# Second layer's gate and up weights in 2 MB tiles, and the context's last expert sums moved into the second layer

## The chip, the cores and the metric

The kernel runs on one core of a Trainium2 chip. The metric is the device time of one execution in microseconds (us); lower is better. Before the change the median of three runs is 1419.86 us (1418.0 to 1425.77). Five engines take part: TensorE (PE in the profile, its weight loads PEld), VectorE (DVE), ScalarE (ACT), GpSimd (POOL) and SyncE (SP), which issues most DMAs.

## The reference, cut to what matters

Two layers over 512 latent tokens and 256 context tokens of width 1024. Each layer normalises, projects, runs three kinds of heads, projects back, and then runs 16 experts, each of which picks 64 latent and (in the first layer alone) 32 context tokens. The second layer doesn't update the context: it only reads it, in its input projection.

```python
def ec_ffn(h, router_w, w_gate, w_up, w_down):
    n_tok, d = h.shape[1], h.shape[2]
    cap = EC_CAPACITY_FACTOR * n_tok // N_EXPERTS
    aff = jax.nn.softmax((h @ router_w).astype(jnp.float32), axis=-1)
    top_aff, idx = lax.top_k(jnp.swapaxes(aff, 1, 2), cap)
    xg = jax.vmap(lambda hb, ib: hb[ib])(h, idx)
    hid = jax.nn.silu(jnp.einsum('becd,edf->becf', xg, w_gate)) * jnp.einsum('becd,edf->becf', xg, w_up)
    y = jnp.einsum('becf,efd->becd', hid, w_down) * top_aff[..., None].astype(h.dtype)
    return jax.vmap(lambda yb, ib: jnp.zeros((n_tok, d), yb.dtype).at[ib.reshape(-1)].add(yb.reshape(-1, d)))(y, idx)

def hybrid_layer(xl, xc, ...):
    hl = rmsnorm(xl, norm1_g) * (1 + sc1) + sh1
    hc = rmsnorm(xc, norm1_g) * (1 + csc1) + csh1
    l_cq, l_ckv, ... = split_columns(hl @ w_in)
    c_cq, c_ckv, ... = split_columns(hc @ w_in)
    ...                                             # heads, w_o, gated residual
    xl = xl + g2 * ec_ffn(rmsnorm(xl, norm2_g) * (1 + sc2) + sh2, router_w, w_gate, w_up, w_down)
    if update_ctx:
        xc = xc + cg2 * ec_ffn(rmsnorm(xc, norm2_g) * (1 + csc2) + csh2, ...)
    return xl, xc
```

All is float32. An expert's gate and up weights are 1024 x 512 each (2 MB), its down weights 512 x 1024 (2 MB), so a layer's experts read 96 MB.

## The kernel before

**Stages of a layer.** Norm and transposed columns of the input (`hcols`), 15 input projections of 128 columns (`proj`, weights split into two parts of reduced precision by `win`), attention, output projection with routing (`wo_half`, `route_half`), then a loop over 16 experts. PE's order is the order of the code; the other engines' instructions are placed by a list scheduler.

**Weight tiles.** All weights pass through one cycle of tiles of 1 MB (8 KB a partition), handed out in turn by `slot`: three always (`ringa`), more in stages where memory is free. The second layer's experts have 3 + 9 (`RING_B`, from the end of attention) + 7 (`RING_D`, from the end of the output projection) = 19 of them. A gate or up matrix takes two tiles, a down matrix two, an expert six. A tile is loaded again as soon as its last reader is done; the loads stand in SP's queue in a fixed order, and a load whose tile isn't free holds up those behind it. In the second layer the down weights of expert 1 are issued by POOL.

**The expert loop.** Pass e of the loop runs, on PE: gates and ups of expert e (`gate_up`, 32 matmuls, gate and up of the same 128 rows in turn), the transposes of the hidden values of expert e-1, in even passes the transposes of gathered rows (`columns`), eight `cb` matmuls that add an earlier pair of experts to the latents, and `down` of expert e-1. POOL gathers the rows of two experts at once (`xg<-tabx`, one buffer).

**From the first layer to the second.** Experts 14 and 15 of the first layer are summed from memory on the chip, not with a DMA: eight pieces of the latents (`cb<-yp`) and four of the context (`cb<-yc`). Their context outputs are collected in a tile `y`, which `split` cuts into two parts `yc`. Then the second layer normalises its six blocks of 128 tokens, latents (2 to 5) before context (0 and 1), `L302` to `L309`: ACT squares and sums, DVE scales and adds epsilon (`rs_t`), POOL takes the power -1/2 (`rs_r`), DVE multiplies (`xt`, `xc`). `first_blocks` (`L369`) follows: per step of 128 rows two column groups (a transpose on PE into one of two `tp` buffers, scale and shift on ACT, a split into two parts) and six matmuls of the first two projections. The sixteen column groups are eight of the latents and eight of the context.

Of the kernel before, what the change touches and what calls it, by code (L numbers as in the profile page):

```python
# [9 lines left out]
F32 = mybir.dt.float32  # L10
# [9 lines left out]
D = 1024  # L20
# [16 lines left out]
RING_B = (3, 9)  # L37
RING_D = (8, 7)
# [6 lines left out]
def hybrid_kernel(ctx: ExitStack, tc: tile.TileContext, a, out):  # L45
# [36 lines left out]
    def more_slots(es, name, n, before, **kw):  # L82

        p = pool(es, name, n, **kw)
        at = len(cycle) - before
        cycle[at:at] = [p] * n
        return p

    def fewer_slots(p):
        cycle[:] = [c for c in cycle if c is not p]  # L90
# [144 lines left out]
    def layer(li, ada):  # L235
# [40 lines left out]
        with ExitStack() as es2:  # L276
# [25 lines left out]
            for tb in order:  # L302
                src = xt[tb]
                if not upd:
                    src = X["xc"][tb] if tb < CB else X["xl"][tb - CB]
                sq = small.tile([128, 1], F32, name="ssq")
                S.activation(hT[1][:, 0:2, 0:512], src.rearrange("p (a b) -> p a b", a=2), AF.Square, accum_out=sq)
                r = rstd_of(sq, 1, 1.0 / D)
                V.tensor_scalar(xt[tb], src, r[:, 0:1], None, op0=OP.mult)  # L309
            outs = pool(es_o, f"outs{li}", side="right")  # L310
# [57 lines left out]

            def first_blocks():  # L369
# [18 lines left out]
            first_blocks()  # L388
# [351 lines left out]
        if upd:  # L740
            xp = pool(xres, "xl", side="right")
            X["xl"] = [xp.tile([128, D], F32, name=f"xl{i}") for i in range(4)]
            X["xces"] = ExitStack()
            xp = pool(X["xces"], "xc", side="right")
            X["xc"] = [xp.tile([128, D], F32, name=f"xc{i}") for i in range(2)]
            for n, src in (("xl", "x"), ("xc", "ctx")):
                for i, t in enumerate(X[n]):
                    Q.dma_start(t, a[src][i * 128:(i + 1) * 128, :])
        es_b = ExitStack()
        ringb = more_slots(es_b, f"ringb{li}", RING_B[li], 3, side="right")  # L750
# [4 lines left out]
        def load_gu(e, q=Q):  # L755
            wgu = wgus[e] = []
            for w in ("exp_w_gate", "exp_w_up"):
                ws = []
                for k in range(0, KD, 4):
                    t = slot([128, 4, FF])  # L760
                    q.dma_start(t, a[w][li, e, k // 4])
                    ws += [t[:, i] for i in range(4)]
                wgu.append(ws)
# [198 lines left out]
        ringd = more_slots(es_d, f"ringd{li}", RING_D[li], len(cycle))  # L962
# [94 lines left out]
        def down(e, r):  # L1057
# [34 lines left out]
            if e == in_dram:  # L1092
                Y[r] = ex.tile([128, D], F32, name=f"y{r}", bufs=1)
            for q in range(np_):
                V.scalar_tensor_tensor(Y[r][i * rows:(i + 1) * rows, q * n:(q + 1) * n], ps[rows * q:rows * (q + 1), :n],
# [3 lines left out]
        def places(r, g):  # L1099

            nt = NL if r == 0 else NCX
            pl = ex.tile([128, nt], F32R, name=f"pl{r}", bufs=2 - r)
# [3 lines left out]
        def split(g):  # L1106

            o = [ex.tile([128, D], F32R, name=f"yc{i}", bufs=1)[64:128] for i in range(2)]
            parts(Y[1][64:128], o, S.copy)
            pl = places(1, g)[64:128]  # L1110
            return [(pl, [y[:, hf * 512:(hf + 1) * 512] for hf in range(2)]) for y in o]

        def combine(r, terms):

            def piece(tb, hf):
# [3 lines left out]
                x = X["xl" if r == 0 else "xc"][tb][:, hf * 512:(hf + 1) * 512]  # L1119
                V.tensor_tensor(x, x, ps, op=OP.add)  # L1120

            for tb in range(len(streams[r])):
# [8 lines left out]
        def finish(e, r):  # L1131
# [77 lines left out]
        fewer_slots(ringb)  # L1209
        fewer_slots(ringd)  # L1210
# [21 lines left out]
def arrays_of(inputs):  # L1232
# [77 lines left out]
```

## Time and profile before

| | us |
|---|---|
| median of three runs | 1419.86 |
| the profiled execution | 1423.59 |
| its span, first to last instruction | 1421.8 |
| PE busy | 1278.7 (90% of the span) |
| DVE busy | 704.3 (50%) |
| ACT busy | 512.0 (36%) |

Around the span lie 1.8 us. PE is the busiest engine, but a busy PE in this profile is not a PE at its peak, and the two places that the change touches have other limits: one is the passage between the layers (about 820 to 860 us from the span's start), the other the second layer's experts (about 1184 us to the end), where the DMA engines are busy throughout.

### The profile page before, as it was taken

To read this page: it belongs to the slowest core of one execution; us is meant where nothing else is said; L and a number is where in the kernel's file an instruction comes from. 1 tells how busy PE (TensorE), PEld (TensorE's weight loads), DVE (VectorE), ACT (ScalarE), POOL (GpSimd) and SP (SyncE) were. 2 spreads that over 40 slices of the span, in tenths; PEclk is the share of its full clock that TensorE was granted. 3 is DMA by queue.
4 is the path that set the end of the run, shared out by engine and by line. 5 is a ranking of instruction groups with operands and counts; after the bars stand their busy time and mean duration, and the time that the engine had idled before them with its cause. 6 is when DMAs were issued, how large, how long until landed. Compare 5 with 4: busy or idle time off the path is not lost. (4 is left out here: it accounts for less than half of the span.)

```text
span 1421.8 us, 21561 instructions
## 1 busy us (share of the span) xinstructions
PE 1278.7 (90%) x8582; PEld 809.6 (57%) x8582; DVE 704.3 (50%) x1554; ACT 512.0 (36%) x1089; POOL 216.4 (15%) x252
## 2 busy tenths in 40 slices
PE   3989989989999959999999969989999968999995
PEld 0768866657678833444444348876778754343332
DVE  1545256566753452333333473847776351333345
ACT  2523145454543322222222252436666332232222
POOL 1111000313120230111111121101232011111111
PEclk9989999999999969999999969998999989999998
DMA  9523416435661398999999811110016458999993
GB/s 362 191 89 119 146 55 235 180 137 188 258 242 43 151 315 325 381 373 378 373 375 376 335 58 59 45 63 1 2 37 254 170 198 322 419 420 419 420 421 121
DMA packets 54309, 321.95 MB, mean 226 GB/s; under 512 B 8561, under 2 KB 8689, under 8 KB 20673
## 3 DMA queue, kind: packets, MB, share of 16 engines
q1 hardware_dynamic: 45664, 286.75, 51.6%
q0 software_dynamic: 8544, 33.82, 7.5%
q8 instruction: 68, 1.11, 0.3%
q14 instruction: 33, 0.26, 0.1%
HBM read 304.52 MB, written 16.02 MB: 225 GB/s over the span
## 5 line engine op out<-in xcount | busy, mean ns | idle before, releaser
L59 PE MATMUL mm<-slot,xgT 128*32 128x256 f32 (+1 forms) x2048 | 290.9, 494 | 4.3 <-DMA slot<-in_exp_w_up_dram 3.6
L59 PE MATMUL mm<-hT,w 128*128 128x512 f32 (+1 forms) x1176 | 230.3, 355 | 3.1 <-POOL w L135 2.0
L59 PEld LDWEIGHTS mm<-hT,w 128*128 128x128 f32 x1176 | 192.2, 192 | 37.4 <-POOL w L135 2.4
L59 PEld LDWEIGHTS mm<-slot,xgT 128*32 128x32 f32 (+1 forms) x2048 | 104.4, 125 | 178.2 <-issue 143.9
L59 PE MATMUL mm<-slot,hTe 128*32 128x256 f32 (+1 forms) x1024 | 147.0, 489 | 1.2 <-ACT hTe L1053 1.1
L1044 DVE TENSOR_TENSOR gh<-mm,gh 64x512 f32<-64x512 f32 (+1 forms) x48 | 29.0, 604 | 189.2 <-ACT gh L1043 187.7
L1043 ACT ACTIVATE gh<-mm 64x512 f32<-64x512 f32 (+1 forms) x48 | 24.9, 519 | 243.3 <-PE mm L59 155.9
L1013 ACT ACTIVATE xgT<-tp,modT,a 128x64 f32<-128x64 f32 (+1 forms) x192 | 68.9, 426 | 85.7 <-PE tp L1009 82.6
L59 PE MATMUL mm<-wo,mixb 128*128 128x512 f32 x360 | 97.5, 406 | 2.3 <-DVE mixb L135 1.3
L59 PEld LDWEIGHTS mm<-slot,hTe 128*32 128x32 f32 (+1 forms) x1024 | 50.2, 123 | 80.6 <-issue 65.6
L689 ACT COPY pt<-tp 128x512 f32<-128x512 f32 (+1 forms) x120 | 64.9, 542 | 82.9 <-PE tp L686 81.9
L686 PE MATMUL tp<-ident,p 128*128 128x128 f32 x552 | 87.8, 284 | 5.8 <-ACT pt L689 2.6
L676 POOL TENSOR_SCALAR p<-p,sm 128x768 f32<-128x768 f32 (+1 forms) x30 | 58.5, 1950 | 125.8 <-DVE sm L675 117.5
L686 PEld LDWEIGHTS tp<-ident,p 128*128 128x128 f32 x552 | 61.6, 142 | 27.4 <-issue 18.3
L59 PE MATMUL ada<-slot,sT 128*32 128x512 f32 x384 | 53.5, 676 | 23.0 <-DMA slot<-in_ada_w_dram 23.0
L59 PEld LDWEIGHTS mm<-wo,mixb 128*128 128x128 f32 x360 | 64.2, 189 | 16.5 <-DVE mixb L135 2.2
L59 PE MATMUL sc<-kt,qh 96*128 96x512 f32 (+1 forms) x324 | 69.7, 348 | 0.0
L59 PE MATMUL sc<-kst,qst 128*128 128x256 f32 (+1 forms) x288 | 49.4, 304 | 20.4 <-DVE mx L673 12.8
L1120 DVE TENSOR_TENSOR xl<-xl,cb 128x512 f32<-128x512 f32 x72 | 45.8, 683 | 44.4 <-PE cb L59 43.4
L134 ACT CAST w<-slot 128x1024 fp32r<-128x1024 f32 x30 | 31.4, 1047 | 100.1 <-PE mm L59 73.8
L665 DVE TENSOR_REDUCE mx<-sc 128x1 f32<-128x768 f32 (+1 forms) x60 | 51.1, 851 | 26.9 <-PE sc L59 25.9
L996 POOL DMA_INDIRECT xg<-tabx,gidx x24 | 23.2, 968 | 254.9 <-PE tp L1051 150.6
(246 smaller groups left out, 1788.0 us busy)
## 6 DMA issues: line engine op xcount, KB each, us to landing
slot<-in_exp_w_gate_dram SPq DMA_DIRECT2D x62, 1024.0 KB, 18.4
slot<-in_exp_w_up_dram SPq DMA_DIRECT2D x62, 1024.0 KB, 17.6
slot<-in_exp_w_down_dram SPq DMA_DIRECT2D x62, 1024.0 KB, 19.8
slot<-in_ada_w_dram SPq DMA_DIRECT2D x48, 1024.0 KB, 6.7
slot<-in_win_dram SPq DMA_DIRECT2D x14, 1024.0 KB, 7.4
slot<-in_wo_dram SPq DMA_DIRECT2D x8, 1024.0 KB, 4.8
tabx<-xn POOLq DMA_DIRECT2D x10, 512.0 KB, 3.0
xt<-in_x_dram SPq DMA_DIRECT2D x4, 512.0 KB, 4.4
```

The lines of the kernel that those rows point to most:

```text
L59: PE.matmul(o, l, r, start=start, stop=stop, skip_group_check=True)
L134: (hi or V.tensor_copy)(out[0], x)
L665: V.tensor_reduce(mx, sc[:, :n], axis=AX.X, op=OP.max, negate=True)
L676: (G if s and self.kind == "mla" else V).tensor_scalar(p[:, :n], p[:, :n], sm, None, op0=OP.mult)
L686: PE.transpose(ps[:, b * 128:(b + 1) * 128], p[:, (b0 + b) * 128:(b0 + b + 1) * 128], ident)
L689: S.copy(o, ps[:, :n * 128])
L996: G.indirect_dma_start(out=xg, out_offset=None, in_=tabx[li], in_offset=bass.IndirectOffsetOnAxis(ap=gidx[:ng, c:c + 1], axis=0))
L1013: S.activation(xgT[:, k0 + k, :n], ps[:, k * ng:k * ng + n], AF.Identity, bias=b[:, 0:1], scale=s[:, 0:1])
L1043: S.activation(gh[64:128, :n], ps[0:64, :n], AF.Silu)
L1044: V.tensor_tensor(gh[0:64, :n], ps[64:128, :n], gh[64:128, :n], op=OP.mult)
L1120: V.tensor_tensor(x, x, ps, op=OP.add)
```

## The change

Two things change. In the second layer a gate or up matrix is one DMA of 2 MB into a tile of 16 KB a partition, out of a copy of the weights in that layout; these tiles come from a cycle of their own (`wide_slot`), four from the end of attention and two more from the end of the output projection. Down weights and all others stay in 1 MB tiles, of which the second layer's experts now have 3 + 1 + 3. Memory for weights is the same: 19 x 8 KB before, 7 x 8 KB + 6 x 16 KB after. The first layer's experts are left as they were.

The four context pieces of experts 14 and 15 leave the end of the first layer. They run between the steps of the second layer's first two latent projections (`first_latents`), followed by the context's norms; the eight context column groups come after these projections instead of between their steps. The second part of these two projections' weights is formed by DVE and no longer by POOL.

```diff
-RING_B = (3, 9)
-RING_D = (8, 7)
+RING_B = ((3, 0), (1, 4))
+RING_D = ((8, 0), (3, 2))
...
+    def wide_slot(shape):
+        wide.append(wide.pop(0))
+        return wide[-1].tile(shape, F32, name="wslot", tag="wslot")
...
-            for tb in order:
+            def norm(tb, junk):
                 src = xt[tb]
                 if not upd:
                     src = X["xc"][tb] if tb < CB else X["xl"][tb - CB]
                 sq = small.tile([128, 1], F32, name="ssq")
-                S.activation(hT[1][:, 0:2, 0:512], src.rearrange("p (a b) -> p a b", a=2), AF.Square, accum_out=sq)
+                S.activation(junk, src.rearrange("p (a b) -> p a b", a=2), AF.Square, accum_out=sq)
                 r = rstd_of(sq, 1, 1.0 / D)
                 V.tensor_scalar(xt[tb], src, r[:, 0:1], None, op0=OP.mult)
+            for tb in order if upd else order[:4]:
+                norm(tb, hT[1][:, 0:2, 0:512])
...
+            def ctx_sums():
+                def start():
+                    S.copy(X["yc"][0][64:128], X["y"][64:128])
+                    V.tensor_tensor(X["yc"][1][64:128], X["y"][64:128], X["yc"][0][64:128].bitcast(F32), op=OP.subtract)
+                def piece(tb, hf):
+                    ps, cs = psn("ada"), slice(hf * 512, hf * 512 + 512)
+                    for i, y in enumerate(X["yc"]):
+                        mm(ps, X["pl"][64:128, tb * 128:(tb + 1) * 128], y[64:128, cs], i == 0, i == 1)
+                    x = X["xc"][tb][:, cs]
+                    V.tensor_tensor(x, x, ps, op=OP.add)
+                def end():
+                    for tb in range(CB):
+                        norm(tb, tmp(D, "junk").rearrange("p (a b) -> p a b", a=2))
+                return [start] + [lambda tb=tb, hf=hf: piece(tb, hf) for tb in range(CB) for hf in range(2)] + [end]
+            def first_latents():
+                hcols(0, NCX, NT, 0)
+                hcols(0, NCX, NT, 1)
+                ws = [win(i) for i in range(2)]
+                pl = [ps_mm() for _ in ws]
+                sums = ctx_sums()
+                for k in range(KD):
+                    if k + 2 < KD:
+                        hcols(0, NCX, NT, k + 2)
+                    for w, ps in zip(ws, pl):
+                        proj_k(ps, w, k, NCX, NT)
+                    for f in sums[k - 1:k] if k else ():
+                        f()
+                for k in range(KD):
+                    hcols(1, 0, NCX, k)
+                first.update({i: [pl[i], None] for i in range(2)})
...
-            first_blocks()
+            (first_blocks if upd else first_latents)()
...
+            X["y"] = xp.tile([128, D], F32, name="y1")
+            X["yc"] = [xp.tile([128, D], F32R, name=f"yc{i}") for i in range(2)]
+            X["pl"] = xp.tile([128, NCX], F32R, name="pl1")
...
+                if not upd:
+                    t = wide_slot([128, KD, FF])
+                    q.dma_start(t, a[w + "1"][e])
+                    wgu.append([t[:, i] for i in range(KD)])
+                    continue
...
-        def split(g):
-            o = [ex.tile([128, D], F32R, name=f"yc{i}", bufs=1)[64:128] for i in range(2)]
-            parts(Y[1][64:128], o, S.copy)
-            pl = places(1, g)[64:128]
-            return [(pl, [y[:, hf * 512:(hf + 1) * 512] for hf in range(2)]) for y in o]
...
-                    todo.extend(combine(0, pair[-2:]))
-            elif e % 4 == 3:
-                todo.extend(combine(1, split(e // 4)))
+                    todo.extend(combine(pair[-2:]))
+            elif e == NE - 1:
+                places(1, e // 4)
...
+    for n in ("exp_w_gate", "exp_w_up"):
+        a[n + "1"] = i[n][1].reshape(NE, KD, 128, FF).transpose(0, 2, 1, 3)
+        a[n] = a[n][:1]
```

The schedule shows what this moves. First DVE, at the passage between the layers, before and after (`xl` and `xt` are latents, `xc` context, `yc` the parts of the context's sums, `w` projection weights). Before:

```order
L135 TENSOR_TENSOR yc_7059<-y_7014,yc_7058 64x1024
L1120 TENSOR_TENSOR xc_3845<-xc_3845,cb 128x512 x2
L1120 TENSOR_TENSOR xc_3846<-xc_3846,cb 128x512 x2
L141 TENSOR_SCALAR rs_t<-ssq 128x1
L309 TENSOR_SCALAR xt_7139<-xl_3838,rs_r 128x1024
L141 TENSOR_SCALAR rs_t<-ssq 128x1
L309 TENSOR_SCALAR xt_7140<-xl_3839,rs_r 128x1024
```

And after, from the same point, which is the latents' last sum:

```order
L152 TENSOR_SCALAR rs_t<-ssq 128x1
L387 TENSOR_TENSOR yc_3849<-y_3847,yc_3848 64x1024
L320 TENSOR_SCALAR xt_7121<-xl_3838,rs_r 128x1024
L152 TENSOR_SCALAR rs_t<-ssq 128x1
L146 TENSOR_TENSOR w_7192<-slot,w_7191 128x1024
L320 TENSOR_SCALAR xt_7122<-xl_3839,rs_r 128x1024
L146 TENSOR_TENSOR w_7196<-slot,w_7195 128x1024
L152 TENSOR_SCALAR rs_t<-ssq 128x1 x2
L320 TENSOR_SCALAR xt_7123<-xl_3840,rs_r 128x1024
L320 TENSOR_SCALAR xt_7124<-xl_3841,rs_r 128x1024
```

The four context sums no longer stand ahead of the latents' norms; the split of `y` and the two weight splits stand among them.

Next ACT, after the column groups of the latents (`ht<-tp` with 512 columns). `ht<-tp` with 256 columns is a column group of the context, `hT<-ht` its first part, `sqq<-mm` reads a finished projection. Before:

```order
L330 ACTIVATE ht<-tp,modT_1508,a_1_2560 128x256 x2
L134 CAST hT_7135<-ht 128x256 x2
L330 ACTIVATE ht<-tp,modT_1508,a_1_2560 128x256 x2
L134 CAST hT_7135<-ht 128x256 x2
L134 CAST w_7400<-slot 128x1024
L393 ACTIVATE sqq_7391<-mm 128x512
```

And after:

```order
L318 ACTIVATE junk,ssq<-xc_3846 128x1024
L444 ACTIVATE sqq_7393<-mm 128x512
L145 CAST w_7402<-slot 128x1024
L344 ACTIVATE ht<-tp,modT_1508,a_1_2560 128x256 x2
L444 ACTIVATE sqq_7394<-mm 128x512
L145 CAST hT_7117<-ht 128x256 x2
L145 CAST w_7461<-slot 128x1024
L344 ACTIVATE ht<-tp,modT_1508,a_1_2560 128x256 x2
L145 CAST hT_7117<-ht 128x256 x2
L344 ACTIVATE ht<-tp,modT_1508,a_1_2560 128x256 x2
```

All eight context groups now stand behind the finished first projection (`sqq`), with the casts of the next two projections' weights between them; before, they were done when it finished.

Last SP, the loads of the second layer's experts from expert 1's on (`slot` is a 1 MB tile, `wslot` a 2 MB tile, `g2l` the gates of the residual). Before:

```order
L761 DMA slot<-in_exp_w_gate_dram 128x2048
L761 DMA slot<-in_exp_w_up_dram 128x2048
L761 DMA slot<-in_exp_w_gate_dram 128x2048 x2
L761 DMA slot<-in_exp_w_up_dram 128x2048 x2
L761 DMA slot<-in_exp_w_gate_dram 128x2048
L984 DMA g2l<-modrow_87 64x512 x2
L761 DMA slot<-in_exp_w_up_dram 128x2048
L769 DMA slot<-in_exp_w_down_dram 128x2048 x3
```

And after:

```order
L830 DMA slot<-in_exp_w_down_dram 128x2048 x2
L817 DMA wslot<-in_exp_w_up_dram 128x4096
L830 DMA slot<-in_exp_w_down_dram 128x2048 x2
L817 DMA wslot<-in_exp_w_gate_dram 128x4096
L817 DMA wslot<-in_exp_w_up_dram 128x4096
L830 DMA slot<-in_exp_w_down_dram 128x2048
L1046 DMA g2l<-modrow_87 64x512 x2
L817 DMA wslot<-in_exp_w_gate_dram 128x4096
L817 DMA wslot<-in_exp_w_up_dram 128x4096
L830 DMA slot<-in_exp_w_down_dram 128x2048
```

Before, four gates' and ups' tiles of experts 2 and 3 could follow one another as tiles came free; now expert 2's down weights stand ahead of its gates, and one down tile of expert 3 stands on either side of that expert's gates and ups.

## Rows read from the trace of the kernel before

**Rows 1.** Windows; stretch, length, engines' busy us, PE clock, DMA share, GB/s.

```profile
600.00:800.00 200.00, 195.74 (x1760) 83.83 (x1758) 75.25 (x182) 46.62 (x132) 25.10 (x21) 1.00 1.02 377
842.00:844.00 2.00, 2.00 (x9) 1.70 (x8) 1.59 (x3) 0.07 (x2) 0.00 (x0) 0.50 0.00 0
1200.00:1350.00 150.00, 145.86 (x688) 57.76 (x683) 53.21 (x80) 40.69 (x91) 18.00 (x14) 0.99 1.01 420
```

**Rows 2.** PE in order of time, between the layers: start, us, work, idle before.

```profile
839.60 3.44 PE L59 MATMUL mm<-hT,w 128*128 128x512 f32 x6
...
846.80 1.62 PE L59 MATMUL mm<-hT,w 128*128 128x512 f32 x6
...
858.80 16.50 PE L59 MATMUL mm<-hT,w 128*128 128x512 f32 x94 [0.53 <-DVE w L135]
```

**Rows 3.** DVE in order of time, between the layers.

```profile
820.85 0.69 DVE L1120 TENSOR_TENSOR xl<-xl,cb 128x512 f32<-128x512 f32 x1 [0.17 <-PE cb L59]
821.57 1.22 DVE L135 TENSOR_TENSOR yc<-y,yc 64x1024 fp32r<-64x1024 f32 x1
823.38 2.63 DVE L1120 TENSOR_TENSOR xc<-xc,cb 128x512 f32<-128x512 f32 x4 [0.59 <-PE cb L59]
...
826.76 2.84 DVE L309 TENSOR_SCALAR xt<-xl,rs_r 128x1024 f32<-128x1024 f32 x1 [0.69 <-POOL rs_r L142]
...
833.89 0.75 DVE L309 TENSOR_SCALAR xt<-xl,rs_r 128x1024 f32<-128x1024 f32 x1 [0.67 <-POOL rs_r L142]
```

**Rows 4.** POOL in order of time, between the layers.

```profile
826.72 2.33 POOL L135 TENSOR_TENSOR w<-slot,w 128x1024 fp32r<-128x1024 f32 x1
```

**Rows 5.** ACT in order of time, between the layers.

```profile
854.65 1.02 ACT L330 ACTIVATE ht<-tp,modT,a 128x256 f32<-128x256 f32 x2 [0.25 <-DVE hT L135]
855.57 0.71 ACT L134 CAST hT<-ht 128x256 fp32r<-128x256 f32 x2
...
858.36 1.05 ACT L134 CAST w<-slot 128x1024 fp32r<-128x1024 f32 x1
```

**Rows 6.** PE's waits in the second layer's experts: us in total, times, longest.

```profile
PE mm L59 <- DMA slot<-in_exp_w_up_dram: 3.6, 2, 3.0
```

**Rows 7.** PE in order of time, second layer's experts.

```profile
1182.77 1.06 PE L1009 MATMUL tp<-ident,xg 128*128 128x128 f32 x8 [1.79 <-DMA xg<-tabx,gidx]
1183.95 13.95 PE L59 MATMUL mm<-slot,xgT 128*64 128x512 f32 x64
...
1199.37 3.65 PE L59 MATMUL mm<-slot,hTe 128*64 128x512 f32 x16
...
1340.24 8.45 PE L59 MATMUL mm<-slot,xgT 128*64 128x512 f32 x30 [3.00 <-DMA slot<-in_exp_w_up_dram]
...
1370.11 7.08 PE L59 MATMUL mm<-slot,xgT 128*64 128x512 f32 x30 [0.58 <-DMA slot<-in_exp_w_up_dram]
...
1383.17 7.04 PE L59 MATMUL mm<-slot,xgT 128*64 128x512 f32 x32
```

**Rows 8.** DMA queues from 1200 to 1350: packets, MB, share of 16 engines.

```profile
q1 hardware_dynamic: 8203, 59.72, 95.8%
q0 software_dynamic: 864, 3.15, 5.2%
```

**Rows 9.** Windows: four stretches of 4 us at the experts' start.

```profile
1186.00:1190.00 4.00, 4.00 (x20) 1.29 (x18) 0.00 (x0) 1.62 (x2) 0.00 (x0) 1.00 0.65 226
1190.00:1194.00 4.00, 4.00 (x22) 1.42 (x20) 0.69 (x1) 0.59 (x1) 0.00 (x0) 1.00 1.00 412
1194.00:1198.00 4.00, 4.00 (x22) 1.19 (x19) 0.00 (x0) 0.00 (x0) 0.00 (x0) 1.00 0.98 332
1198.00:1202.00 4.00, 3.95 (x25) 1.93 (x26) 0.69 (x1) 3.65 (x10) 0.96 (x1) 1.00 0.93 381
```

**Rows 10.** SP in order of time: the first load after a tile came free.

```profile
1187.63 0.34 SPq L761 DMA_DIRECT2D slot<-in_exp_w_up_dram  x1
```

**Rows 11.** The gathers of the second layer, from issue to landing.

```profile
DMA to landing us min/median/max: 4.3/8.6/8.9
```

More of the change, by code (lines that the diff above doesn't have):

```diff
@@ L80, in slot, with more_slots @@
         return cycle[-1].tile(shape, F32, name="slot", tag="slot")
-    def more_slots(es, name, n, before, **kw):
+    wide = []
+    def wide_slot(shape):
+        wide.append(wide.pop(0))
+        return wide[-1].tile(shape, F32, name="wslot", tag="wslot")
+    def more_slots(es, name, n, before, cyc=cycle, **kw):
+        if not n:
+            return None
         p = pool(es, name, n, **kw)
-        at = len(cycle) - before
-        cycle[at:at] = [p] * n
+        at = len(cyc) - before
+        cyc[at:at] = [p] * n
         return p
     def fewer_slots(p):
-        cycle[:] = [c for c in cycle if c is not p]
+        for cyc in cycle, wide:
+            cyc[:] = [c for c in cyc if c is not p]
     def psn(tag):
@@ L749, in layer @@
         es_b = ExitStack()
-        ringb = more_slots(es_b, f"ringb{li}", RING_B[li], 3, side="right")
+        rings = [more_slots(es_b, f"ringb{li}", RING_B[li][0], 3, side="right"),
+                 more_slots(es_b, f"wideb{li}", RING_B[li][1], 0, wide, side="right")]
         load_wo(1, 1)
@@ L961, in layer @@
         es_d = ExitStack()
-        ringd = more_slots(es_d, f"ringd{li}", RING_D[li], len(cycle))
+        rings += [more_slots(es_d, f"ringd{li}", RING_D[li][0], len(cycle)),
+                  more_slots(es_d, f"wided{li}", RING_D[li][1], len(wide), wide)]
         steps[0]()
@@ L1091, in down @@
             i = e % np_
-            if e == in_dram:
-                Y[r] = ex.tile([128, D], F32, name=f"y{r}", bufs=1)
             for q in range(np_):
-                V.scalar_tensor_tensor(Y[r][i * rows:(i + 1) * rows, q * n:(q + 1) * n], ps[rows * q:rows * (q + 1), :n],
+                V.scalar_tensor_tensor(X["y"][i * rows:(i + 1) * rows, q * n:(q + 1) * n], ps[rows * q:rows * (q + 1), :n],
                                        gw[r][rows * q:rows * (q + 1), e:e + 1], g2[r][rows * q:rows * (q + 1), :],
@@ L1101, in places, with combine @@
             nt = NL if r == 0 else NCX
-            pl = ex.tile([128, nt], F32R, name=f"pl{r}", bufs=2 - r)
+            pl = X["pl"] if r else ex.tile([128, nt], F32R, name=f"pl{r}", bufs=2)
             G.tensor_scalar(pl, tok[:, :nt], slots[r][:, g:g + 1], None, op0=OP.is_equal)
             return pl
-        def split(g):
-            o = [ex.tile([128, D], F32R, name=f"yc{i}", bufs=1)[64:128] for i in range(2)]
-            parts(Y[1][64:128], o, S.copy)
-            pl = places(1, g)[64:128]
-            return [(pl, [y[:, hf * 512:(hf + 1) * 512] for hf in range(2)]) for y in o]
-        def combine(r, terms):
+        def combine(terms):
             def piece(tb, hf):
@@ L1118, in piece @@
                     mm(ps, pl[:, tb * 128:(tb + 1) * 128], ys[hf], i == 0, i == len(terms) - 1)
-                x = X["xl" if r == 0 else "xc"][tb][:, hf * 512:(hf + 1) * 512]
+                x = X["xl"][tb][:, hf * 512:(hf + 1) * 512]
                 V.tensor_tensor(x, x, ps, op=OP.add)
-            for tb in range(len(streams[r])):
+            for tb in range(len(streams[0])):
                 for hf in range(2):
@@ L1208, in layer @@
         es_d.close()
-        fewer_slots(ringb)
-        fewer_slots(ringd)
+        for p in rings:
+            fewer_slots(p)
     ada = []
```

## The prediction

> **What bounds the kernel now.** I read the windows by stage first. The second layer's experts (about 1184 us to the end) have both PE and the DMA engines busy: 145.86 of 150 us on PE, and the DMA engines without a gap at 420 GB/s [rows 1]. PE's waits tell which of the two sets the end: only 3.6 us of waiting for weights in the whole stage, in two waits [rows 6]. PE in order of time shows them at 1340.24 (3.00 us, the gates and ups of expert 12) and at 1370.11 (0.58 us, expert 14); expert 15 starts at 1383.17 without one [rows 7]. So PE sets the pace first, lives on a stock of loaded tiles, and from expert 12 on has none left: PE and DMA end level. The weights arrive at 2.49 us a MB there: expert 12 and expert 14 lie 12 MB apart, and 1370.11 - 1340.24 = 29.87 us. Anything that makes the weights late by more than a microsecond is paid in full at the end; anything that makes them early is worth no more than the two waits, 3.6 us, plus the 1.8 us by which the 30 matmuls after the longer one ran slow (8.45 us against about 6.6, which is 7.04 for 32 scaled down) [rows 7].
>
> The other place is the passage between the layers. DVE adds the latents' last sum at 820.85, and PE has its first projection at 839.60; between lie context sums and norms, one after the other on DVE [rows 2, 3]. From 858.80 on PE runs 94 matmuls without a gap [rows 2]: this is the point at which a gain or loss of the passage is read.
>
> **The change part by part: the passage.** The latents' last sum ends at 821.5, and the four context adds follow from 823.38 [rows 3]. In place of these DVE does, by the new order, a share of the norms at once: the split of the context's sums and two weight splits of the same size at 1.22 each, four norms at 0.75, and small statistics between them, which I put at 0.15 each: 7.3 us, and some 0.6 us for POOL's power. The norms count 0.75 each, not 2.84: the first two of before ran beside POOL's weight split of 2.33 us, which is gone, and the third, without one, took 0.75 [rows 3, 4]. The last latent norm ends at 829.4. The transposes, ACT's column group and DVE's two parts add 2.4 us: first projection at 831.8, 7.8 us earlier than 839.60.
>
> What follows takes that back. The loop has the same 48 matmuls, 0.27 us each (1.62 for six) [rows 2], 13.0 us; six latent column groups of four transposes at about 0.36, 2.2 us; the eight moved context matmuls at 0.27, 2.2 us; and the start at low clock (0.50, the lower of the two levels, while PE was busy all through 842 to 844 [rows 1]; six matmuls 3.44 us there against 1.62 [rows 2]), some 1.3 us: end at 850.5. Before, the loop ended at about 857.5 with all context columns in it. Now they come behind it, alone, through two PSUM buffers. Before the last two find a buffer, ACT's order holds: two weight casts at 1.0, three pairs of groups at 1.0, two pairs of their casts at 0.7 [rows 5], two squares put at 0.5: 7.4 us. PE's stream of the next projection, queued behind these transposes, starts at about 857.9 instead of 858.4 (858.80 less two matmuls that ran earlier), and after 7 us with little work PE starts it at the lower clock: up to 1.8 us. Less about 1.1 us because the clock rises sooner at the start of the loop, this comes to +0.2, and I take 0. Bounds: -6 (the head start of 7.8 kept, less some 2 for the moved matmuls) and +4 (the low clock lasting as it did from 836 to 844, half of 8 us).
>
> **The change part by part: the second layer's experts.** Work on PE, DVE and ACT is the same; the loads differ.
>
> First gather. Tiles for 19 MB stand ready in both versions before expert 0 is through. Before, 12 MB of loads stand ahead of the tiles that come free with the output projection, and 7 MB behind; by the new order 10 ahead (expert 2's down weights stop the queue) and 9 behind. The 2 MB more, 5.0 us at 2.49, are still moving when POOL gathers the first rows. A gather lands after 4.3 us at least and 8.6 in the median [rows 11]; PE waited for this one at 1182.77 [rows 7]. Cost 0 to 4.3; I take 2.
>
> Restart. After the 19 MB the DMA engines stand idle until a tile comes free. Before, that is when half of expert 0's gates and ups is done: SP issues at 1187.63 [rows 10]. The four stretches up to 1202 moved 226, 412, 332 and 381 GB/s [rows 9], as much as 12.9 us at 420, so it is as if a full stream had begun at 1189.1. Now both 2 MB tiles come free when expert 0 is through: 1183.95 + half of 13.95 = 1190.9 [rows 7], plus the 2 of the gather and 0.5 to start: 1193.4. Its 4 MB last 10 us; the next load, a down tile, waits for the first half of expert 0's down matmuls (1199.37 + 1.8 + 2 = 1203.2 [rows 7]), and what is queued behind it on SP, expert 4's gates and ups, waits with it: the stream just holds.
>
> Whole tiles. Counted from the order, before, the first half of expert 14's ups is MB 87 of the stage; the whole of expert 15's ups, which PE now needs before its first matmul, is MB 94 in the new order. Before, MB 87 less the 19 took 1370.11 - 1189.1 = 181.0 us; seven more at 2.49 are 17.4.
>
> Rate. The two queues give two equations: 8203 packets and 59.72 MB took 95.8% of 16 x 150 us, 864 packets and 3.15 MB 5.2% [rows 8]. Their solution is 37.4 us a MB and 8.2 ns a packet. A 2 MB tile saves 144 packets, 0.074 us of 4.99 over 16 engines, 1.5%; the 24 tiles of experts 4 to 15 save 1.8 us. Bounds: no gain, if the packets keep their size; at most 3.6 us, if all 190 us went at 428 GB/s (16 / 37.4); and a loss, for which the nearest row is the first layer's 377 GB/s [rows 1], a stage with scatters beside the loads: 10% on 190 us would be 19 us. Nothing in the change adds such traffic, so I keep only 4 us of loss. The Trainium skill (HBM Reference, Specifications) puts a core that streams alone at about 425 GB/s. By that ceiling the 190 us could shrink by 1.2%, 2.3 us, not 3.6; this trace's 420 lies just under it.
>
> Sum: 1193.4 + 181.0 + 17.4 - 1.8 = 1390.0, less 1.3 for a gather of 0.5 MB that now falls into the idle time = 1388.7, against 1383.17: +5.5. PE's short waits (about 1 us an expert from the tenth on) cost it clock inside time that it waits anyway. Behind expert 15's start nothing changes; its down weights land 5 us later and are needed 15.7 us later.
>
> The sum goes against the profiled execution: 1423.59 + 0 + 5.5 = 1429.1. That execution lies 3.7 us above the median of 1419.86, so I forecast 1425.
>
> **The rivals.**
> *The head start is kept* (-6 + 5.5): 1419. For it: DVE and PE really are through with the latents 6 to 8 us earlier. Against it: ACT's order above, with all eight context groups behind the first finished projection.
> *The weights are never late.* If packets of twice the size bring enough, both waits go: -5.4, 1414.5; with the head start 1409. For it: only 3.6 us of waiting stand between. Against it: the packet's share of 8.2 ns. The Trainium skill (DMA: Bandwidth & Descriptors, Bandwidth) gives 341 GB/s for a DMA of 1 MB and 425 for 16 MB, by which larger DMAs would gain far more; the 2.49 us a MB shows 420 with 1 MB tiles, so that loss isn't there to win.
> *The DMA engines start late* and the kernel gets slower. The first gather lands under full load (8.6): 2.3 more; PE, without work for over 4 us, then runs expert 0 at the lower clock, 1.8 more, and its tiles come free that much later; with no gain in rate, 1.8. 1425 + 5.9 = 1431. It decides from the point at which expert 0's gates and ups end 3 us later than by the sum, apart from what the passage shifts. For it: the 9 MB behind the output projection; against it: the gather shares the engines only for its last part.
>
> **How the numbers follow.** Forecast 0.52 (own range 1420 to 1429), head start kept 0.18, never late 0.09, late start 0.21. A measurement of this kernel tells about 0.5%, 7.1 us, from no change: faster is below 1412.8, slower above 1427.0. Faster: most of never late with some head start, 0.08. Slower: late start 0.19, and the upper part of the forecast, 0.14: 0.33. The rest, 0.59, is within. For 8 in 10 the range goes from the never-late case to above the late start: 1414 to 1434.
>
> **What would show it.** The first projection starts near 832 and the long stream behind the context's columns still near 858; if it begins near 852, the passage's step fails. The DMA engines idle from the landing of the first 19 MB until expert 0's gates and ups end; windows beyond 1210 at 425 to 427 GB/s; PE's waits for gates and ups add to 6 to 9 us in short pieces from expert 10 or 11 on. Windows still at 420 or below, or waits that begin at expert 8 or earlier, would make the forecast too low; no waits at all, too high.

## The result, and the profile after

The changed kernel takes 1435.45 us (median of 4 runs, 1430.7 to 1439.24), the kernel before beside it 1422.13 (4 runs): a ratio of 1.0092, 95% interval 1.0066 to 1.0119. It is slower, by some 13 us, and the forecast of 1425 and its range, 1414 to 1434, both lie below it. The direction and the DMA rate that were named came; the size did not. The profiled execution took 1430.7 us, the fastest of the four, with a span of 1428.9 us.

Executions of one kernel differ by some us before the changed places are reached. So times of the passage are counted below from the end of the latents' last sum on DVE, and times inside the experts from the choice: the two PE transposes of the lists of chosen rows (`tp<-ident,lt`), at 1176.00 in the profile before and at 1174.72 after. Prices of kernels are ratios, put into us at 1421.5.

The passage, PE in order of time (start, us, work, idle time before and its releaser); it answers to [rows 2]:

```profile
830.43 3.02 PE L60 MATMUL mm<-hT,w 128*128 128x512 f32 x6
...
849.12 0.27 PE L342 MATMUL tp<-ident,xc 128*128 128x128 f32 x1
850.60 0.55 PE L342 MATMUL tp<-ident,xc 128*128 128x128 f32 x3 [1.20 <-DVE xc L320]
851.58 1.15 PE L342 MATMUL tp<-ident,xc 128*128 128x128 f32 x4 [0.44 <-ACT ht L344]
854.53 1.15 PE L342 MATMUL tp<-ident,xc 128*128 128x128 f32 x4 [1.81 <-ACT ht L344]
856.40 1.15 PE L342 MATMUL tp<-ident,xc 128*128 128x128 f32 x4 [0.72 <-ACT ht L344]
857.20 19.22 PE L60 MATMUL mm<-hT,w 128*128 128x512 f32 x96
```

The latents' last sum, the zero of this stage, ends at 815.01 + 4.87 = 819.88 (before, at 821.5):

```profile
815.01 4.87 DVE L1173 TENSOR_TENSOR xl<-xl,cb 128x512 f32<-128x512 f32 x8
```

The head start is there: the first projection comes 10.6 us after that sum, not 18.1. The context's columns take it back, waiting for ACT. A window shows what PE pays for that (columns as in [rows 1]):

```profile
852.00:862.00 10.00, 7.47 (x22) 5.29 (x22) 5.25 (x11) 6.77 (x16) 0.00 (x0) 0.50 0.54 210
```

The granted clock is at its lower level from 852 to 862; 96 matmuls take 19.22 us, where 94 took 16.50 [rows 2].

The experts' start, PE, answering to [rows 7]:

```profile
1174.72 0.39 PE L983 MATMUL tp<-ident,lt 16*128 16x16 f32 x2 [11.70 <-DVE lt L979]
...
1183.28 1.94 PE L1071 MATMUL tp<-ident,xg 128*128 128x128 f32 x8 [2.81 <-DMA xg<-tabx,gidx]
1185.15 14.51 PE L60 MATMUL mm<-wslot,xgT 128*64 128x512 f32 x64
```

From the choice to expert 0's columns it is 8.56 us, not 6.77. POOL in order of time says why. First before, then after (no row of either stands ahead of the prediction):

```profile
1163.00 0.58 POOL L858 DMA_DIRECT2D tabx<-xn  x1 [1.49 <-DMA slot<-in_exp_w_gate_dram]
1163.61 1.08 POOL L769 DMA_DIRECT2D slot<-in_exp_w_down_dram  x2
1177.55 1.06 POOL L996 DMA_INDIRECT xg<-tabx,gidx  x1 [12.27 <-DVE gw L939]
```

```profile
1156.11 0.54 POOL L830 DMA_DIRECT2D slot<-in_exp_w_down_dram  x1 [1.92 <-PE tp L928]
...
1159.38 0.58 POOL L830 DMA_DIRECT2D slot<-in_exp_w_down_dram  x1
1160.89 0.54 POOL L919 DMA_DIRECT2D tabx<-xn  x1 [0.93 <-ACT xn L917]
...
1178.92 1.06 POOL L1058 DMA_INDIRECT xg<-tabx,gidx  x1 [16.91 <-issue]
```

`tabx` is the table in DRAM from which rows are gathered; its last 512 KB are written here. Expert 1's two down loads, which POOL issued behind that write, now stand ahead of it. How long the four writes of the stage took to land, before and after:

```profile
DMA to landing us min/median/max: 2.9/3.0/9.2
```

```profile
DMA to landing us min/median/max: 2.9/3.0/17.2
```

The last write lands at 1160.89 + 17.2 = 1178.1, after the choice, and the gather is issued 4.20 us after the choice instead of 1.55. That the gather waited for this write is read from these times; the profile names no releaser (`issue`), and an experiment below tests it. It then lands in 4.2 us (before, 5.1):

```profile
xg<-tabx,gidx POOLq DMA_INDIRECT x1, 4.2
```

SP's first load of a tile that came free, and the windows (for [rows 9, 10, 1]):

```profile
1192.82 0.34 SPq L817 DMA_DIRECT2D wslot<-in_exp_w_gate_dram  x1
```

```profile
1190.00:1194.00 4.00, 4.00 (x22) 1.35 (x20) 0.51 (x1) 0.59 (x1) 0.00 (x0) 1.00 0.18 33
1194.00:1198.00 4.00, 4.00 (x22) 1.32 (x20) 0.18 (x1) 0.00 (x0) 0.00 (x0) 1.00 0.87 340
1198.00:1202.00 4.00, 3.95 (x24) 1.80 (x22) 0.69 (x1) 1.89 (x5) 0.66 (x1) 1.00 1.01 434
1202.00:1210.00 8.00, 8.00 (x40) 2.73 (x38) 2.12 (x3) 3.10 (x8) 0.30 (x1) 1.00 0.99 383
1210.00:1350.00 140.00, 135.92 (x634) 53.55 (x632) 50.86 (x76) 36.44 (x80) 17.43 (x13) 1.00 1.01 425
```

The DMA engines stand nearly idle until expert 0 is through (33 GB/s) and then run at 425 GB/s, but not at once: 340 from 1194 to 1198 and 383 from 1202 to 1210. The queues [rows 8] and PE's waits [rows 6], and the waits in order of time from the first:

```profile
q1 hardware_dynamic: 5495, 60.12, 95.3%
q0 software_dynamic: 864, 3.15, 5.3%
```

```profile
PE mm L60 <- DMA wslot<-in_exp_w_up_dram: 5.1, 6, 1.5
```

```profile
1299.08 7.08 PE L60 MATMUL mm<-wslot,xgT 128*64 128x512 f32 x30 [0.81 <-DMA wslot<-in_exp_w_up_dram]
...
1388.52 1.02 PE L60 MATMUL mm<-wslot,xgT 128*64 128x512 f32 x2
1390.23 7.08 PE L60 MATMUL mm<-wslot,xgT 128*64 128x512 f32 x30 [0.69 <-DMA wslot<-in_exp_w_up_dram]
```

From expert 9 on every expert except expert 14 waits a little. Expert 15's gates and ups end 222.59 us after the choice (1390.23 + 7.08 - 1174.72); before it was 214.21.

### The profile page after: what moved, and what is told of

It reads as the page before. It is cut to its first block, busy times and chain, and to the rows that moved or that the text cites. A ratio compares the mean times of both kernels' runs of the same rounds, so it can differ in the third digit from the quotient of the medians.

```text
span 1428.9 us, 21486 instructions
## 1 busy us (share of the span) xinstructions
PE 1282.0 (90%) x8582; PEld 808.7 (57%) x8582; DVE 702.8 (49%) x1556; ACT 511.3 (36%) x1089; POOL 213.6 (15%) x250
## 5 line engine op out<-in xcount | busy, mean ns | idle before, releaser
L60 PE MATMUL mm<-slot,xgT 128*32 128x256 f32 (+1 forms) x1536 | 173.0, 452 | 1.3 <-DVE xgT L1077 0.7
L60 PE MATMUL mm<-wslot,xgT 128*64 128x512 f32 x512 | 120.3, 596 | 5.1 <-DMA wslot<-in_exp_w_up_dram 5.1
L60 PEld LDWEIGHTS mm<-slot,xgT 128*32 128x32 f32 (+1 forms) x1536 | 66.4, 119 | 98.3 <-issue 70.5
L60 PE MATMUL mm<-wo,mixb 128*128 128x512 f32 x360 | 101.6, 420 | 1.6 <-ACT mixb L145 0.9
L60 PEld LDWEIGHTS mm<-wslot,xgT 128*64 128x64 f32 x512 | 38.0, 138 | 84.5 <-issue 71.9
L60 PEld LDWEIGHTS mm<-wo,mixb 128*128 128x128 f32 x360 | 67.5, 198 | 16.5 <-ACT mixb L145 1.4
## 6 DMA issues: line engine op xcount, KB each, us to landing
slot<-in_exp_w_up_dram SPq DMA_DIRECT2D x30, 1024.0 KB, 14.2
```

The source lines that it names most:

```text
L60: PE.matmul(o, l, r, start=start, stop=stop, skip_group_check=True)
```

## The experiments

The theory after the first comparison had three parts: the passage, whole 2 MB tiles, and the first gather. Its rival for the gather was the prediction's own argument, the 9 MB of loads. All kernels were timed in five rounds beside the kernel before, on three chips, so they are compared by their ratios. "Restart" is SP's first load of a freed tile, "end" the end of expert 15's gates and ups, both in us from the choice, from each kernel's profile.

| kernel | ratio to before, 95% | us | restart | end |
|---|---|---|---|---|
| before | | | 11.6 | 214.21 |
| changed, again | 1.0084 (1.0061 to 1.0108) | +11.9 | 19.0 | 223.42 |
| passage alone | 1.0016 (1.0001 to 1.0031) | +2.3 | 11.6 | 213.67 |
| whole tiles alone | 1.0052 (1.0033 to 1.0071) | +7.4 | 18.8 | 223.54 |
| half tiles alone | 1.0018 (0.9999 to 1.0036) | +2.6 | 14.9 | 216.91 |
| changed, table write by ACT | 1.0057 (1.0039 to 1.0074) | +8.1 | 14.2 | 218.49 |
| half tiles, table write by ACT | 1.0001 (0.9984 to 1.0019) | +0.1 | 10.9 | 211.23 |
| before, table write by ACT | 1.0002 (0.9984 to 1.0020) | +0.3 | 10.8 | 213.04 |
| changed, half tiles and write by ACT | 1.0011 (0.9993 to 1.0030) | +1.6 | 10.8 | 212.67 |
| half tiles, two loads each | 1.0010 (0.9990 to 1.0030) | +1.4 | 11.2 | 214.17 |

**The changed kernel once more**, with no edit.

> The changed kernel once more, for its time on the same chip as the parts and a second trace. If the parts add up: the sum of the two others within 3 us, about +8 to +13 on before. If its trace is again near 1429 us in span while the timed runs lie near 1435, the difference is between executions and not in the two places; if it is near 1435, the stretch that is longer than in the first trace shows where.

1434.35 us (6 runs). The loss is there again, and so is the held gather: its columns start 9.23 us after the choice.

**The passage alone** (against the changed kernel):

```diff
-RING_B = ((3, 0), (1, 4))
-RING_D = ((8, 0), (3, 2))
+RING_B = ((3, 0), (9, 0))
+RING_D = ((8, 0), (7, 0))
...
-                if not upd:
-                    t = wide_slot([128, KD, FF])
-                    q.dma_start(t, a[w + "1"][e])
-                    wgu.append([t[:, i] for i in range(KD)])
-                    continue
```

> The passage alone: the context's last sums and norms are moved as in the change, all weights stay in 1 MB tiles as before. Theory A (the time is lost in the second layer's experts, by late and whole 2 MB tiles, and the passage costs little: the trace of the changed kernel has it 2.8 us longer from the latents' last sum to the end of the second layer's third projection): +1 to +4 us on before. Rival B (the passage is what costs, by context columns alone on ACT and a PE at the low clock behind them): +8 to +13 us. Rival C (the passage is a gain that the experts hide): -2 us or less.

1423.88 us (12 runs). A small loss, just told from none; the experts run as before. The latents' last sum, the passage's zero, ends here at 817.21 + 1.28 = 818.49:

```profile
817.21 1.28 DVE L1168 TENSOR_TENSOR xl<-xl,cb 128x512 f32<-128x512 f32 x2 [0.17 <-PE cb L60]
```

**Whole tiles alone**, on the passage of before (against the kernel before):

```diff
-RING_B = (3, 9)
-RING_D = (8, 7)
+RING_B = ((3, 0), (1, 4))
+RING_D = ((8, 0), (3, 2))
...
+                if not upd:
+                    t = wide_slot([128, KD, FF])
+                    q.dma_start(t, a[w + "1"][e])
```

> The 2 MB tiles alone: weights of the second layer's gates and ups as in the change, the passage as before. Theory A: +6 to +10 us on before; expert 15 starts some 7 us later, counted from the end of the routing, as in the changed kernel. Rival B: +0 to +4 us. Rival C: +9 us or more, more than the whole change.

1429.91 us (8 runs). Most of the loss is here, and the gather is held here too (columns 9.07 us after the choice), so that the cause lies with the tiles and not with the passage.

**Half tiles alone**: 2 MB tiles again, but each with one half of the rows of both gates and ups (against whole tiles alone):

```diff
-                    q.dma_start(t, a[w + "1"][e])
+                    t = wide_slot([128, 2, 4, FF])
+                    q.dma_start(t, a["exp_w_gu1"][e, h])
```

> 2 MB tiles of 16 KB a partition cut the other way: one tile holds rows 0 to 511 of both gate and up, the next rows 512 to 1023 of both; passage as before. PE can start on the first tile and frees it halfway, as with 1 MB tiles. Theory A (lateness by whole tiles costs, the packets of 16 KB are a small gain): 3 to 6 us less than the 2 MB tiles alone, so +0 to +5 us on before. Rival D (the order and number of loads ahead of the first gather cost, not the whole tiles): the same as the 2 MB tiles alone, within 2 us.

1424.39 us (12 runs): 4.8 us less than whole tiles by the ratios. What is left, 2.6, goes with a gather still held (columns 8.60 us after the choice).

**The table's last write by ACT.** In the changed kernel this edit takes the write out of POOL's queue and leaves the order of the weights' loads as it is:

```diff
-                G.dma_start(tabx[li][row:row + 128, :], xn)
+                (S if not upd and tb == tbs[-1] else G).dma_start(tabx[li][row:row + 128, :], xn)
```

> The changed kernel with one difference: the last write of the second layer's table of rows (512 KB, the table from which the experts' rows are gathered) is issued by ACT, which made the rows, and so no longer stands behind expert 1's two down loads on POOL's queue. Theory A (the order on POOL's queue holds the first gather back: 17.2 us from issue to landing of that write against 9.2 before): the write lands 3 to 9 us after its issue, the first gather is issued about 1.6 us after the transposes of the choice's rows instead of 4.2, expert 0's columns start 6.8 us after them instead of 8.6 to 9.2, expert 2 starts 27 to 28 us after them instead of 29.9 to 30.8, and the kernel ends 2 to 3 us earlier than the changed one: 1431.5 to 1433. Theory B (it is the 9 MB of loads behind the output projection, as the prediction had it): the write or the gather lands as late as now whatever its queue, expert 0 starts no earlier, and the time stays within 1 us of the changed kernel's 1434.4.

1429.09 us (11 runs): 3.8 to 5.0 less than the changed kernel's two measurements, by the ratios. The intervals of the ratios touch (1.0039 to 1.0074 here, 1.0061 to 1.0108 there), so the size is loose; the profiles carry the argument. Theory A's mechanism holds; its 2 to 3 us look too low. POOL and then PE in this kernel:

```profile
1180.17 1.06 POOL L1058 DMA_INDIRECT xg<-tabx,gidx  x1 [14.90 <-DVE gw L1000]
```

```profile
1178.63 0.39 PE L983 MATMUL tp<-ident,lt 16*128 16x16 f32 x2 [11.70 <-DVE lt L979]
...
1184.54 1.07 PE L1071 MATMUL tp<-ident,xg 128*128 128x128 f32 x8 [0.76 <-DMA xg<-tabx,gidx]
1185.72 13.96 PE L60 MATMUL mm<-wslot,xgT 128*64 128x512 f32 x64
```

The gather is issued 1.54 us after the choice, and its columns start after 5.91 us, earlier than before the change, with the same loads behind the output projection. So these loads, by their amount, were not what held it. Nor were they more than before. SP's loads around the end of the output projection, before the change and in the changed kernel:

```profile
1157.94 0.80 SPq L761 DMA_DIRECT2D slot<-in_exp_w_gate_dram  x2
1158.80 1.25 SPq L761 DMA_DIRECT2D slot<-in_exp_w_up_dram  x2
1160.10 0.47 SPq L761 DMA_DIRECT2D slot<-in_exp_w_gate_dram  x1
```

```profile
1125.84 3.60 SPq L830 DMA_DIRECT2D slot<-in_exp_w_down_dram  x2
1155.84 0.33 SPq L817 DMA_DIRECT2D wslot<-in_exp_w_gate_dram  x1
1156.26 0.38 SPq L817 DMA_DIRECT2D wslot<-in_exp_w_up_dram  x1
1156.70 0.42 SPq L830 DMA_DIRECT2D slot<-in_exp_w_down_dram  x1
```

Five 1 MB loads before; two of 2 MB and one of 1 MB after. With POOL's two that makes 7 MB behind the output projection in both kernels. Expert 2's down weights, which the prediction counted among them, went out at 1125.84, some 30 us earlier.

The restart comes 3.9 us earlier (14.2 against 18.1), and the end 4.1 (218.49 against 222.59): what the gather loses is paid in full.

The same edit on half tiles alone:

> The kernel with 2 MB tiles that hold half the rows of gates and ups together, on the passage of before, and with the last table write issued by ACT. Theory A: the same 2 to 3 us come off it as off the changed kernel, 1424.4 to about 1421.5 to 1422.5, level with the kernel before. Theory B: it stays at 1424.4.

1420.96 us (12 runs): level with the kernel before, and 2.4 less than half tiles alone by the ratios, whose intervals overlap; the end comes 5.7 us earlier in the profile (211.23 against 216.91).

And on the kernel before, as a control:

> Control: the kernel before with the same edit, the last table write issued by ACT instead of POOL. There that write stands ahead of expert 1's down loads on POOL's queue and the first gather is issued 1.55 us after the choice's transposes, not held back. Theory A (the 5 us that this edit took off the changed kernel were the change's own cost, made by the new order on POOL's queue): nothing to win here, the time stays within 1.5 us of 1421.4. Theory B (the write is dear on POOL's queue in any order): 2 to 5 us faster.

1422.17 us (11 runs), nothing won: the write was cheap on POOL's queue until loads stood ahead of it.

**Half tiles filled by two loads** (against half tiles alone; same tiles, same order on POOL, packets of 8 KB):

```diff
-                    q.dma_start(t, a["exp_w_gu1"][e, h])
+                    for s in range(2):
+                        q.dma_start(t[:, s], a["exp_w_gu1"][e, h][:, s])
```

> The kernel with half tiles, but each 2 MB tile filled by two loads of 1 MB, so that a packet is 8 KB as before while tiles, slots and waits stay. Theory A (the rate comes from the packets' size): 420 GB/s again in the experts' windows instead of 425, some 1.5 to 2 us more at the end than with half tiles alone: about 1426. Theory B (it comes from fewer loads on the queue or from the tiles): 425 stays, 1424.4.

1423.30 us (12 runs). Neither theory's time came, and the time does not tell, since two effects oppose each other; the profiles tell. The window from 1210 to 1350, half tiles first:

```profile
1210.00:1350.00 140.00, 137.41 (x654) 55.50 (x656) 54.09 (x81) 36.94 (x82) 20.29 (x15) 1.00 1.01 422
```

```profile
1210.00:1350.00 140.00, 137.57 (x652) 56.33 (x652) 53.53 (x81) 37.45 (x82) 18.78 (x14) 1.00 1.01 419
```

The rate falls, as theory A said, though by 3 GB/s rather than 5. The other profiles agree: in this stretch the seven kernels with one load a 2 MB tile stand at 422 to 425, and the kernels before, passage alone, before with the write by ACT and this one, all with 1 MB loads, at 419 to 420. So the gain does not come from the tiles; whether it is the packets' size or the number of loads, no run separates. But the gather is issued early (1.64 us after the choice, 4.20 with one load), with expert 1's down loads still ahead of the table's write. Those two loads' and then the four writes' landing, half tiles first:

```profile
DMA to landing us min/median/max: 12.3/13.9/15.6
DMA to landing us min/median/max: 2.9/3.0/17.0
```

```profile
DMA to landing us min/median/max: 9.8/10.8/11.8
DMA to landing us min/median/max: 2.9/3.0/14.2
```

The order on POOL's queue is the same; the packets on SP's queue are half as large and the loads twice as many. Beside 16 KB packets POOL's loads and write land 2.5 to 3.8 us later. So POOL's order alone did not hold the gather; it did so together with the larger packets.

Packets, MB and engine share of both queues over 4 us in which both are full, half tiles (1164 to 1168) first, then with two loads (1169 to 1173):

```profile
q1 hardware_dynamic: 75, 1.23, 71.6%
q0 software_dynamic: 76, 0.49, 29.2%
```

```profile
q1 hardware_dynamic: 112, 0.79, 50.6%
q0 software_dynamic: 103, 0.77, 49.2%
```

The two queues move about as many packets each, whatever the packets' size; so SP's queue (q1) gets 2.5 times POOL's bytes with 16 KB packets, and as many as POOL's with 8 KB.

**The passage with PE kept at work**: transposes of the unit matrix behind each of the context's eight column groups, into PSUM that nobody reads; eight of them, then three (against the passage alone):

```diff
                 for k in range(KD):
                     hcols(1, 0, NCX, k)
+                    ps = psn("ada")
+                    for i in range(8):
+                        PE.transpose(ps[:, i % 4 * 128:i % 4 * 128 + 128], ident, ident)
```

> The changed passage alone, with weights as before, and eight transposes of the unit matrix on PE behind each column group of the context, into PSUM that nobody reads, so that PE has work while it waits for ACT. Theory A (what the passage costs is the low clock after the thinly used stretch: 96 matmuls in 19.2 us against 94 in 16.5): the granted clock stays at 1.00, the stream takes about 16.9 us, and the kernel ends 1.5 to 2.4 us earlier than with the changed passage alone: 1421.5 to 1422.5. Theory B (the cost is the later start behind ACT's order, or there is none): the start and the time stay where they are, 1423.9, or get later by the added matmuls.

1423.58 us (12 runs), ratio 1.0005 (0.9982 to 1.0028). The clock stays up, but the stream starts 10.5 us after the first context transpose (8.1 with the passage alone): given away again.

> The changed passage alone with three transposes of the unit matrix, not eight, behind each column group of the context. Eight kept the granted clock at 1.00 but took the groups from about 1.0 to 1.15 us each, so that the next projection started later. Theory A (the low clock costs 1.5 to 2.4 us and eight were too many): the clock stays at 1.00, the groups keep their pace, 1421.5 to 1422.5. Theory B (three are too few to keep the clock, or the passage's cost is its later start): as with the passage alone, 1423.5 to 1424.

1422.43 us (12 runs), ratio 0.9999 (0.9983 to 1.0016). Three are enough for the clock. The stream in the passage alone, and with three:

```profile
854.59 18.52 PE L60 MATMUL mm<-hT,w 128*128 128x512 f32 x96
```

```profile
859.07 16.94 PE L60 MATMUL mm<-hT,w 128*128 128x512 f32 x96
```

A window of 2 us in the context's columns, some 5.5 us after the first of them, in the same order:

```profile
852.00:854.00 2.00, 1.27 (x5) 0.71 (x6) 1.42 (x3) 1.75 (x5) 0.00 (x0) 0.50 0.43 66
```

```profile
856.00:858.00 2.00, 1.43 (x11) 1.11 (x11) 1.56 (x3) 1.75 (x6) 0.00 (x0) 1.00 0.24 37
```

1.6 us come back in the stream, and 0.3 is lost before it (8.4 us after the first context transpose). The profile is clear; the time agrees with it, but its interval overlaps that of the passage alone, so that these 1.3 us are shown in the trace only.

**All mends together**: the changed kernel with half tiles and the table's write by ACT.

> The changed kernel with both mends: 2 MB tiles that hold half the rows of gates and ups together, and the last table write issued by ACT. Theory A (whole tiles, the held gather and the passage add up): whole tiles cost 5 to 8 of the 1429.1 of the kernel with the write alone mended, and what stays is the passage: 1422 to 1424. Theory B (the parts do not add; the passage's shift in time keeps some of the loss): 1425 or more.

1423.83 us (12 runs). What is left, 1.6 us (its interval includes no change at all), is put down to the passage. By the ratios the parts are: passage 1.6 and 2.3, whole instead of half tiles 4.8 and 6.5 (on the passage of before, 7.4 - 2.6; on the changed one with the write mended, 8.1 - 1.6), held gather 3.8 to 5.0 on the changed kernel and 2.4 on half tiles (1.0018 against 1.0001). That the steps from this kernel up to the changed one sum to its loss (1.6 + 6.5 + 3.8 = 11.9) holds by construction, since each is the difference of neighbours. The test is the two parts measured alone: passage +2.3 and whole tiles +7.4 (with their held gather) make +9.7, where the changed kernel measured +11.9 and +13.1. The 2 to 3 us between lie within the intervals of these ratios; that the parts add exactly is not shown.

No version beats the kernel before. Half tiles with the write by ACT end expert 15's gates and ups 3.0 us earlier in the trace, but the median is level within 0.2%.

## Why the prediction was wrong

**The base.** 3.7 us were taken off because the profiled execution lay above the median of three runs. With 25 to 34 runs the kernel before stands at 1421.4 to 1422.1, so 1.5 to 2.2 of them were the luck of three runs.

**The passage: ±0, measured +1.6 to +2.3.** Counted from the end of the latents' last sum (821.5 before, 819.88 in the changed kernel, 818.49 in the passage alone), the first projection came after 10.6 us in both kernels (10.3 foretold), the loop's end after 29.2 and 28.0 (29.0, or 27.9 with the 1.1 taken off for a clock that rises sooner), the stream after 37.3 and 36.1 (36.4, or 35.3; before, less its two matmuls, 36.9). The low clock, priced at up to 1.8, cost 19.22 - 16.50 x 96/94 = 2.4 us in the changed kernel and 18.52 - 16.85 = 1.7 in the passage alone. So in the passage alone both clock terms came as priced, and the step that failed is the way from the loop's end to the stream: 8.1 us in both kernels, not 7.4. PE first waits 1.20 there for the context's norm on DVE, which the sum of ACT's work does not have; whether that is the whole 0.7 is not shown. In the changed kernel's first profile the clock rose later (3.02 us for the first six matmuls, 2.47 in the passage alone), so the 1.1 was not won either. From the latents' last sum to the stream's end these two profiles lose 2.8 and 0.9 us.

**The first gather: +2 for expert 0's columns, measured 1.8 and 2.5, by another mechanism.** That the size came is luck. The prediction looked for more loads behind the output projection (9 MB, not 7) that slow the gather; the loads were 7 MB as before, and the gather landed in 4.2 us, not later than before. What came late was its source: two loads stand ahead of the table's last write on POOL's queue, beside larger packets on SP's. The prediction read neither POOL's order nor what SP's packets do to another queue. Before, the write was not late by anything: 9.2 us, 3.8 of them to spare (1163.00 + 9.2 = 1172.2 against the choice at 1176.00). What the sum did not price at all is that PE then runs slowly (from 1184 to 1186, where the columns' transposes end and the experts' matmuls begin, the granted clock is 0.50 in the changed kernel and 1.00 with the write by ACT): the eight transposes took 1.94 us, not 1.06, and the first 64 matmuls 14.51, not 13.95 (15.22 and 15.40 in two others with a held gather, 13.96 with the write by ACT). The prediction had this clock cost only in its late rival.

**The restart: the step that failed at the experts.** The sum has SP's first load 16.9 us after the choice and a full stream 0.5 later. Measured, the load is issued at 18.1, 1.2 later: expert 0's first matmul comes 0.5 later than in the sum, and its gates and ups take 0.7 longer. Then "the stream just holds" failed: up to 1210 the windows moved 33 x 4 + 340 x 4 + 434 x 4 + 383 x 8 = 6.3 MB in 17.2 us, which 425 GB/s would do in 14.8. So the restart cost 2.4 us where 0.5 was priced, although the prediction's own figure for the kernel before was 1.5 (1187.63 to 1189.1). The stream is 3.1 us behind the sum here, and hardly any of it is won back: expert 15's ups, which were to set its start, arrive at 1390.23, 215.5 after the choice, where the sum has 212.7, and the end comes at 222.59 against 212.7 + 7.04 = 219.7. In the second profile it is 223.42. So the experts cost +8.4 and +9.2 where +5.5 was foretold.

**Whole tiles.** The counting of MB and the rate were right: from the stream's start to expert 15's ups the sum has 195.3 us (1388.7 - 1193.4), and measured it is 215.5 - 18.1 - 2.4 = 195.0. With the write by ACT the end is still 218.49 - 214.21 = +4.3, although expert 0's columns start 0.9 earlier there; that is the price of whole tiles and of their restart.

Together: 2.9 to 3.7 too little at the experts, 1.6 to 2.3 at the passage and 1.5 to 2.2 at the base make 6.0 to 8.2 of the some 10 us between 1425 and the two medians. The rest lies within the intervals and stays open.

**Rate.** The estimate from the two queues' shares held: 425 GB/s. PE's waits came in short pieces, but from expert 9 and 5.1 us in all, not from expert 10 or 11 and 6 to 9. The Trainium skill (HBM Reference, Specifications) puts a core that streams alone at about 425 GB/s; the trace's 425 agrees. By that figure larger packets had no more to win here.

**The rivals.** The head start was not kept, for the reason given. The weights are late with whole tiles and, at 3.6 us of waits, also with half tiles and a free gather. The late start (1431) is the nearest to what happened: a price in the gather, a slow expert 0 and a late restart. Its condition, expert 0's gates and ups ending 3 us later than in the sum, was not met (restart 18.1 us after the choice in the changed kernel, 16.9 in the sum), it kept no gain in rate, which came, and its mechanism was wrong.

## What to carry over

When a change frees or fills tiles at other times, read the order of every queue for small transfers that someone waits for, and ask which bulk loads now stand ahead of them. Where matmuls take two operands in turn and a tile holds all rows of one, both tiles (4 MB here) must have landed before PE gets on, and both come free only at the end; tiles of the same size with half the rows of both keep the packets, let PE start after one tile and free it halfway, 4.8 to 6.5 us here. A head start that ended in a thinly used stretch cost the clock of what followed, 1.7 to 2.4 us here. And count a stage's times from one event that both kernels have: taken from the span's start, expert 15's start looked as foretold (1388.52 against 1388.7), while from the choice it was late.

## What the runs showed of the hardware

Two queues share the DMA engines by packets and not by bytes: with SP's packets at 16 KB instead of 8, two 1 MB loads on POOL's queue land after 12.3 and 15.6 us instead of 9.8 and 11.8, and the write behind them after 17.0 instead of 14.2. While both were full the queues moved 75 and 76 packets in 4 us in the one case, 112 and 103 in the other. So the larger packets slow the other queue. Loads of 2 MB with 16 KB packets ran at 422 to 425 GB/s, loads of 1 MB with 8 KB packets at 419 to 420. The Trainium skill (DMA: Bandwidth & Descriptors, Queues, rings and completion order) says that each engine turns from queue to queue packet by packet; the trace agrees, in packets as the profile counts them. This rule, read against the change, would have pointed at POOL's queue.

Three small transposes behind each column group kept PE's granted clock at 1.00 over a stretch where it otherwise fell to 0.50, and cost 0.3 us.
